# Output projections of a two-layer trunk: rows 0 to 3 from full-float products to split products, with two vector operations moved to ScalarE

## The chip, the cores and the metric
The kernel runs on one core of one Trainium2 chip, in one launch. The metric is the device time of one execution in microseconds (us); the number given for a kernel is the median of its runs. Engines: PE is TensorE (PEld its weight loads), DVE is VectorE, ACT is ScalarE, POOL is GpSimd, and SP issues the DMAs.

## The reference, cut to what matters
The input is x of 256 positions by 1024 channels, all in float32. There are two layers, each a mixer and a squared-ReLU MLP with 4096 hidden channels, each behind an RMSNorm and with a residual add.

```
def mixer_ab(h, w_in, conv_w, ln_g, ln_b, w_out):      # layer 0
    u_val, u_gate, q, k, v = split(h @ w_in)           # 512 columns each
    ya = silu(layernorm(causal_conv31(u_val * sigmoid(u_gate)), ln_g, ln_b))
    yb = attention(q, k, v)                            # 8 heads of 64, causal, ALiBi
    return concatenate([ya, yb], -1) @ w_out           # 1024 x 1024

def mixer_c(h, w_in, conv_w, conv_b, ...):             # layer 1
    gate, xr = split(h @ w_in)                         # 1024 columns each
    xr = causal_conv4(xr, conv_w) + conv_b
    r, i = sigmoid(xr @ w_r + b_r), sigmoid(xr @ w_i + b_i)   # block diagonal, 8 x 128
    a = exp(-8 * r * softplus(-lam))
    y = scan(a, sqrt(1 - a * a) * (i * xr)) * gelu(gate)
    return y @ w_out                                   # 1024 x 1024

x = x + mixer(rmsnorm(x));  x = x + (relu(rmsnorm(x) @ w_up) ** 2) @ w_down
```

## The kernel before, in words
Activations lie transposed: a tile holds 128 channels by 256 positions, so that 1024 channels are eight tiles, numbered 0 to 7 (a "row" of a projection is one such tile of its input, and the 128 rows of the weight that belong to it). Weights come from HBM in pieces of 1 MB, two units of 512 KB each. In both output projections rows 0 to 3 are, in layer 0, the convolution's four tiles `y[c]` and, in layer 1, the first four tiles `gi[c]` of the recurrence; rows 4 to 7 of layer 0 are the attention's output.

**Two forms of product.** `mm` (line 685) multiplies one unit's tile with one activation tile. If the weight is a plain float32 tile it is one float32 matmul. If it is a pair (`wh`, `wl`) and the activation a pair (high, low), it is three matmuls of the type fp32r: `wh` by high, `wh` by low, `wl` by high. A pair is made in `weights` (line 565): per half unit a copy `wh<-raw` (128x512, by `move`, which either ACT or DVE can take) and a subtraction `wl<-raw,wh` on DVE. An activation's pair is made in `split_act` (line 708) in the same way, on 128x256.

**Where weights lie.** There are five buffers `raw` (NRAW, a whole piece each) and eight pairs of buffers `wh`/`wl` (NSPL), both used in rotation. `piece` (line 516) gives a piece a place: "raw" stays in a `raw` buffer unsplit; "split" lands in a `raw` buffer and then takes one `wh`/`wl` pair for each of its two units; "pair" lands, unsplit, with its first unit in a `wh` buffer and its second in the `wl` buffer beside it, and needs no `raw`. Before the change rows 4 to 7 of layer 0's output projection are "split", and rows 0 to 3 of it and all eight rows of layer 1's are "pair".

**The order.** Nothing is issued as written. Each call records an operation with its reads, writes and a cost; a planner (`Plan`, line 50 on) then does list scheduling forward and backward for ten rounds, with a model of each engine's costs and of the DMA queue (one rate, DMA_RATE, for all transfers), and the best order by that model is emitted, each engine's queue strictly in that order. The weight DMAs keep the order in which they were written, on SP's queue. PE's order is in the plan, too.

**Around the change.** Layer 0: four tiles of the 31-tap convolution run on DVE beside the projections and the attention; `ln` (line 929) takes mean and variance over channels with matmuls against `ones`, in between the output projection's rows 4 to 7 (`out_rows`), and ends with four Silu on ACT; then `out_cols` (line 961) runs over pairs of output tiles with rows 0 to 3 inside, and calls `residual_chunk` for each finished tile, which starts the MLP's norm. Layer 1: `xr_tail` (line 1099) is the four-tap convolution, `gates`, `recur_a` (line 1119), `recur_b`, `recur_c` are the recurrence, `gate_out` (line 1145) multiplies with the Gelu of the gate and gives `mx[c]`; then `out_rows` for rows 0 to 3 one after another and `out_cols` for rows 4 to 7. The MLP's first six up units (`up0` to `up5`) and its first down units take the `wh`/`wl` pairs that come next in the rotation.

**SBUF.** The eight tiles `xg` (x times the norm's gain, 128x256) are used by layer 0's input projections only.

Of the kernel before, what the change touches and what calls it, by code (L numbers as in the profile page):

```python
# [6 lines left out]
F32 = mybir.dt.float32  # L7
# [4 lines left out]
P = 128  # L12
S = 256
# [315 lines left out]
def hybrid_trunk(ctx, tc, x, mix_norm, mlp_norm, w_up, w_down, ab_w_in, ab_conv_w, ab_ln_g, ab_ln_b,  # L329
# [8 lines left out]
    def tl(name, shape=(P, S), dt=F32):  # L338
        return sb.tile(list(shape), dt, name=name)
# [5 lines left out]
    def act(out, in_, func, scale=1.0, bias=None, accum=None):  # L345
        kw = {}
        ins = [in_]
        c = 0.05 if is_psum(in_) else 0.092
        c += fsize(in_) * 0.000833
        for n, v in (("scale", scale), ("bias", bias)):  # L350
            if isap(v):
                ins.append(v)
                c += 0.093
            if v is not None:
                kw[n] = v
        outs = [out]
        if accum is not None:
            kw["accum_out"] = accum
            outs.append(accum)
            c += 0.093  # L360
        return plan.add("A", [("activation", (out, in_, func), kw)], outs, ins, {"A": c}, func)
# [4 lines left out]
    def tt(out, a, b, op, engs="V"):  # L366
        n = fsize(out)
        cost = {}
        if "V" in engs:
            cost["V"] = vcost(n)  # L370
        if "G" in engs:
            cost["G"] = 0.135 + n * 0.0021
        return plan.add(engs, [("tensor_tensor", (out, a, b), {"op": op})], [out], [a, b], cost)
# [17 lines left out]
    def move(out, a, scale=None):  # L391

        n, ap, far = fsize(out), scale is not None, not is_psum(a)

        def go(e, sub):
            if e is nc.scalar:
                return e.activation(sub(out), sub(a), AF.Copy, **({"scale": scale} if ap else {}))  # L397
            return e.tensor_scalar(sub(out), sub(a), scale, None, op0=OP.mult) if ap else e.tensor_copy(sub(out), sub(a))  # L398

        return plan.add("VA", [(go, (), {})], [out], [a] + ([scale] if ap else []),  # L400
                        {"V": vcost(n, far, ap), "A": (0.092 if far else 0.05) + n * 0.000833 + 0.093 * ap}, AF.Copy)
# [12 lines left out]
    def memset(out, v, engs="G"):  # L414
        return plan.add(engs, [("memset", (out, v), {})], [out], [], {engs: 0.1 + fsize(out) * 0.0005})

    def mms(items, after=()):

        calls, outs, ins, c = [], [], [], 0.0
        for o, l, r, st, sp in items:  # L420
            calls.append(("matmul", (o,), {"lhsT": l, "rhs": r, "start": st, "stop": sp, "skip_group_check": True}))
            outs.append(o)
            ins += [l, r]
            c += max(fsize(r) / 2400.0, 0.0533) * (1 if l.dtype == F32R else 4) + (0.0135 if l.dtype == F32R else 0.005)
        return plan.add("T", calls, outs[:1], ins, {"T": c}, after=after)
# [12 lines left out]

        return plan.add("G", [("dma_start", (out, in_), {})], [out], [in_], {"G": 0.55}, lag=4.0)

    def dma(out, in_, size):
        return plan.add("S", [("dma_start", (out, in_), {})], [out], [in_], {"S": 0.0}, size=size)


    ident = tl("ident", (P, P))
    ones = tl("ones", (P, P))
    pcol = tl("pcol", (P, P))
    wcol = tl("wcol", (P, P))
    eps_t = tl("eps", (P, 1))
# [3 lines left out]

    whs = [tl(f"wh{i}", (P, KD * P)) for i in range(NSPL)]
    wls = [tl(f"wl{i}", (P, KD * P)) for i in range(NSPL)]
    shared = {t.tensor.name: f"{n}{i}" for n, ts_ in (("wh", whs), ("wl", wls)) for i, t in enumerate(ts_)}
    plan.shared = {n: 0 for n in shared}

    def renew(name, form):
        return sb.tile([P, KD * P], F32R if form % 2 else F32, name=f"{shared[name]}_{form}", tag=shared[name])  # L460

    def take(t, part):

# [23 lines left out]
    def rot(tag, n=None, shape=(P, S), dt=F32):  # L487
        if tag not in pools:
            pools[tag] = [[tl(f"{tag}{i}", shape, dt) for i in range(n)], 0]
        p = pools[tag]  # L490
        t = p[0][p[1] % len(p[0])]
        p[1] += 1
        return t
# [45 lines left out]
    def rows(ap, place):  # L539
        return piece("r", ap, place)  # L540
# [4 lines left out]
    def load(n, lo=0, hi=KD):  # L545

        taken[1] = n + 1
        kind, ap = pieces[n]
        for j, home in enumerate(homes[n]):
            if home.tensor.name in shared:  # L550
                take(home, 0)
            if kind == "ri":
                dma(home.rearrange("p (k c) -> p k c", k=KD), (c_w_r, c_w_i)[j][0].rearrange("h i j -> i h j"), P * 4096)
                continue
            if kind == "gv":
                dma(home.rearrange("p (k c) -> p k c", k=KD)[:, lo:hi], ap[j][:, lo:hi], P * 512 * (hi - lo))
                continue
            h = ap.shape[1] // 2
            a, b = (j * h, j * h + h) if kind == "r" else (max(lo, j * h), min(hi, j * h + h))
            if a < b:  # L560
                dst = home.rearrange("p (a b) -> p a b", a=h)
                dma(dst[:, a - j * h:b - j * h], ap[:, a:b], P * 4096 * (b - a) // h)

    @plan.part
    def weights(u):
# [41 lines left out]
    wo = ab_w_out[0].rearrange("(k p) c -> p k c", p=P)  # L607
    u_o = {}
    for k in (4, 6, 0, 2):
        u_o[k], u_o[k + 1] = rows(wo[:, k:k + 2], "split" if k > 3 else "pair")  # L610
    LAG, TAIL = 4, 4

    def mlp_units(layer):
# [16 lines left out]
        u_gt += cols(c_w_in[0], c, "split")  # L630
    wco = c_w_out[0].rearrange("(k p) c -> p k c", p=P)
    for k in range(0, 8, 2):
        u_co += rows(wco[:, k:k + 2], "pair")
    u_up[1], u_dn[1] = mlp_units(1)


# [10 lines left out]
    R = lambda ap: ap.rearrange("a (b p) -> (a b) p", p=P)  # L647
    make_identity(nc, ident)
    memset(ones, 1.0, "V")
    memset(eps_t, EPS, "V")  # L650
    act(tiny[:, 60:61], eps_t, AF.Sqrt)

# [27 lines left out]
    def par(name, c):  # L680
        i = col0[name] + c
        return pcol[:, i:i + 1]
# [21 lines left out]
    def narrow(b, w, xs):  # L704
        for k in range(0, KD, 4):
            mms([(b[:, :S], w[1][:, j, :], xs[j][0], False, j == KD - 1) for j in range(k, k + 4)])

    def split_act(src, scale, tag, bufs, engs="V"):
        t = rot(tag, bufs, (P, 2 * S), F32R)
        h, lo = t[:, :S], t[:, S:]  # L710
        if scale is None:
            move(h, src)
            tt(lo, src, h.bitcast(F32), OP.subtract, engs)
        else:
            move(h, src, scale)
            stt(lo, src, scale, h.bitcast(F32), OP.mult, OP.subtract)
        return h, lo, t

    def scaled(src, scale):
        t = rot("xg", KD)  # L720
        move(t, src, scale)
        return t

    def residual_chunk(k, acc, gname, g0, xs):
        tt(xT[k], acc, xT[k], OP.add)
# [20 lines left out]
    def x_chunk(k):  # L746
        b = bank("a")
        transposes([(b[:, t * P:(t + 1) * P], xrow[k * XP // KD][:, t, k % (KD // XP) * P:(k % (KD // XP) + 1) * P], ident) for t in range(2)])
        xs[k] = scaled(b[:, :S], par("mix", k))
        move(xT[k], b[:, :S])  # L750

    for k in range(KD):
# [175 lines left out]
    @plan.part  # L928
    def ln():
        tt(mean, y[0], y[1], OP.add)  # L930
        tt(mean, mean, y[2], OP.add)
        b = bank("b")
        mms([(b[:, :S], ones, mean, True, False)])
        mms([(b[:, :S], ones, y[3], False, True)])
        act(mean, b[:, :S], AF.Copy, scale=1.0 / 512)
        sq = [ssum, rot("nsq", 2), sumb, rot("nsq", 2)]
        for c in range(4):
            tt(y[c], y[c], mean, OP.subtract)
            act(sq[c], y[c], AF.Square)
            if c % 2:  # L940
                tt(sq[c - 1], sq[c - 1], sq[c], OP.add)
        b = bank("b")
        mms([(b[:, :S], ones, ssum, True, False)])
        mms([(b[:, :S], ones, sumb, False, True)])
        act(mean, b[:, :S], AF.Sqrt, scale=1.0 / 512, bias=eps_t)
        recip(mean, mean)
        for c in range(4):
            tt(y[c], y[c], mean, OP.mult)
            act(y[c], y[c], AF.Silu, scale=par("lng", c), bias=par("lnb", c))
            mx[c] = y[c]  # L950

    def accumulators():
        t = [bank("a") for _ in range(4)]
# [145 lines left out]
    def xr_tail(c, b):  # L1099
        xp = xps[c % 2]  # L1100
        tt(xp[:, 3:], b[:, :S], rstd, OP.mult)
        t = ar(S)
        ts(t, xp[:, 0:S], par("cw", c), par("cb", c), OP.mult, OP.add)
        for j in range(1, 4):
            stt(t, xp[:, j:j + S], par("cw", j * KD + c), t, OP.mult, OP.add)
        xc[c] = t
# [12 lines left out]
    def recur_a(c):  # L1119

        a = arot("ga", 8, S)
        act(a, gr[c], AF.Exp, scale=neg4[:, c:c + 1], bias=neg4[:, c:c + 1])
        act(gr[c], gr[c], AF.Tanh, scale=pos4[:, c:c + 1], bias=pos4[:, c:c + 1])
        a2 = arot("a2", 2, S)
        tt(a2, a, a, OP.mult)
        stt(gr[c], a2, 1.0, gr[c], OP.add, OP.mult)
        stt(gi[c], gi[c], 1.0, xc[c], OP.add, OP.mult)
        ga[c] = a
# [16 lines left out]
    def gate_out(c):  # L1145
        act(ym[c], ym[c], AF.Gelu_apprx_tanh)
        tt(gi[c], ym[c], xc[c], OP.mult)
        mx[c] = gi[c]

    b0, b1 = xr_proj(0), xr_proj(1)  # L1150
    finish_norm()
# [112 lines left out]
```

## Time and profile before

| | |
|---|---|
| median of 3 runs | 568.79 us (568.79 to 569.5) |
| the profiled execution | 569.07 us |
| its span, from first to last instruction | 567.3 us |
| mean granted TensorE clock | 0.998 |
| PE, PEld | 558.9 us (99%), 482.2 us (85%) |
| DVE, ACT | 415.4 us (73%), 310.9 us (55%) |
| HBM read | 97.11 MB |

The busy shares are over the whole span; single stages differ from them. The granted clock is 1.00 in every slice but the last, that is, the 2.4 GHz level. A float32 matmul stands in the trace as two matmul records. Since matmuls are pipelined and their ends are modelled, the durations of single matmuls overlap, and a pace is better read from a stretch of time and a count. Most lines have the number L312, that of the helper that issues recorded operations, so groups are told apart by tiles. ("Identity" and "Square" in the change are functions of ACT's activate instruction.)

### The profile page before, as it was taken

The page shows a single profiled execution, that of the slowest core. Times are in us where ns is not written, and L with a number is a line of the kernel's source. Part 1 is how long each engine was busy: PE and PEld are TensorE (multiplying, and loading weights), DVE is VectorE, ACT ScalarE, POOL GpSimd, SP SyncE. Part 2 cuts the span into 40 slices and gives each one's busy share as a digit, 9 for nine tenths or more (in the row PEclk, how much of TensorE's full clock was granted, in tenths as well). Part 3 has the DMA queues.
Part 4 walks back from the last instruction along what each step waited for, and adds up shares of the span by engine and source line. Part 5 has one row for each costly group of instructions (what it writes and reads, how often), then busy time and mean ns, then how long its engine had stood idle before and what let it go on. Part 6 is the DMA issues. An engine that isn't in the chain of part 4 may idle for free.

```text
span 567.3 us, 8519 instructions
## 1 busy us (share of the span) xinstructions
PE 558.9 (99%) x2985; PEld 482.2 (85%) x2985; DVE 415.4 (73%) x962; ACT 310.9 (55%) x641; POOL 7.5 (1%) x31
## 2 busy tenths in 40 slices
PE   8999999999999999999999999999999999999995
PEld 7887849988888888888889999888888888888884
DVE  2899998889766765776649999869677667757722
ACT  5104134667655656565537797728555655565623
POOL 5000000000000000000000000000000000000000
PEclk9999999999999999999999999999999999999999
DMA  8991493316666566565009738945656665662001
GB/s 241 283 375 73 138 323 134 122 56 193 196 209 192 172 200 197 175 197 174 0 1 278 242 123 280 370 157 156 199 167 191 210 192 172 202 203 93 1 1 75
DMA packets 71739, 98.71 MB, mean 174 GB/s; under 512 B 3368, under 2 KB 59776, under 8 KB 71696
## 3 DMA queue, kind: packets, MB, share of 16 engines
q1 hardware_dynamic: 71408, 98.06, 55.0%
q8 instruction: 23, 0.38, 0.3%
q14 instruction: 20, 0.16, 0.1%
q0 software_dynamic: 288, 0.11, 0.1%
HBM read 97.11 MB, written 1.05 MB: 173 GB/s over the span
## 4 chain that ended last, share of the span: by engine, by line
PE 94%; DMA 3%; DVE 2%; issue 1%; SPq 0%; ACT 0%; DVEq 0%; ACTq 0%
PE bank_b L312 50%; PE bank_a L312 44%; DMA raw<-in_ab_w_out_dram 2%; DVE arena L312 1%; DMA arena<-in_x_dram 1%; DVE wl L312 0%; SPq L312 0%; ACT arena L312 0%; ACT wh L397 0%; DVE xg L398 0%; DVE x L398 0%; DVE x L312 0%; DVE xT L398 0%; ACT tiny L312 0%; DVE tiny L312 0%
## 5 line engine op out<-in xcount | busy, mean ns | idle before, releaser
L312 DVE TENSOR_TENSOR wl<-raw,wh 128x512 fp32r<-128x512 f32 x296 | 197.0, 687 | 97.5 <-PE bank_b L312 75.6
L397 ACT ACTIVATE wh<-raw 128x512 fp32r<-128x512 f32 x265 | 163.8, 629 | 114.7 <-PE bank_a L312 53.7
L312 PE MATMUL bank_b<-x,wh 128*128 128x512 f32 (+1 forms) x768 | 169.7, 356 | 0.0
L312 PE MATMUL bank_a<-wh,f 128*128 128x512 f32 x512 | 158.5, 391 | 0.0
L312 PEld LDWEIGHTS bank_b<-x,wh 128*128 128x128 f32 x768 | 136.3, 189 | 20.3
L312 PEld LDWEIGHTS bank_a<-wh,f 128*128 128x128 f32 x512 | 94.2, 188 | 18.1
L312 PE MATMUL bank_b<-x,wl 128*128 128x256 f32 x640 | 102.6, 283 | 0.0
L312 PE MATMUL bank_a<-wl,f 128*128 128x512 f32 x256 | 99.6, 389 | 0.0
L312 PEld LDWEIGHTS bank_b<-x,wl 128*128 128x128 f32 x640 | 90.2, 191 | 2.5
L312 PEld LDWEIGHTS bank_a<-wl,f 128*128 128x128 f32 x256 | 48.1, 188 | 10.2
L312 DVE SCALAR_TENSOR_TENSOR arena<-arena,wcol 128x256 f32<-128x256 f32 x120 | 50.7, 484 | 0.2
L312 ACT ACTIVATE relu<-bank_b 128x256 f32<-128x256 f32 x64 | 24.5, 383 | 32.0 <-PE bank_b L312 30.4
L312 PE MATMUL bank_b<-xg,raw 128*128 128x256 f32 x160 | 35.8, 380 | 0.0
L312 PEld LDWEIGHTS bank_b<-xg,raw 128*128 128x128 f32 x160 | 29.9, 190 | 3.9
L312 ACT ACTIVATE relu<-relu 128x256 f32<-128x256 f32 x64 | 23.7, 410 | 17.1 <-DVE relu L312 17.0
L312 DVE TENSOR_TENSOR relu<-bank_b,relu 128x256 f32<-128x256 f32 x64 | 26.6, 419 | 3.9 <-ACT relu L312 3.9
L312 ACT ACTIVATE arena<-arena 128x256 f32<-128x256 f32 (+2 forms) x39 | 18.8, 522 | 16.2 <-DVE arena L312 15.6
L312 PE MATMUL bank_a<-arena,wl 128*128 128x256 f32 x96 | 26.3, 379 | 0.0
L312 PE MATMUL bank_a<-arena,wh 128*128 128x256 f32 x96 | 26.3, 379 | 0.0
L312 DVE TENSOR_TENSOR f<-relu,f 128x256 fp32r<-128x256 f32 x64 | 25.3, 419 | 0.5 <-ACT f L397 0.5
L312 DVE SCALAR_TENSOR_TENSOR relu<-relu,rstd 128x256 f32<-128x256 f32 x64 | 24.4, 419 | 0.1
L312 DVE TENSOR_TENSOR xT<-bank_a,xT 128x256 f32<-128x256 f32 x24 | 8.9, 419 | 15.8 <-PE bank_a L312 15.8
(127 smaller groups left out, 443.6 us busy)
## 6 DMA issues: line engine op xcount, KB each, us to landing
raw<-in_w_up_dram SPq DMA_DIRECT2D x64, 512.0 KB, 4.5
raw<-in_w_down_dram SPq DMA_DIRECT2D x64, 512.0 KB, 4.3
raw<-in_c_w_in_dram SPq DMA_DIRECT2D x16, 512.0 KB, 7.0
raw<-in_ab_w_in_dram SPq DMA_DIRECT2D x8, 512.0 KB, 8.1
wh<-in_ab_w_in_dram SPq DMA_DIRECT2D x5, 512.0 KB, 9.2
wl<-in_ab_w_in_dram SPq DMA_DIRECT2D x5, 512.0 KB, 9.6
raw<-in_ab_w_out_dram SPq DMA_DIRECT2D x4, 512.0 KB, 10.5
wh<-in_c_w_out_dram SPq DMA_DIRECT2D x4, 512.0 KB, 3.4
```

The source lines that it names most:

```text
L312: r.append(getattr(self.engines[o.eng], method)(*map(sub, a), **{n: sub(v) for n, v in k.items()}))
L397: return e.activation(sub(out), sub(a), AF.Copy, **({"scale": scale} if ap else {}))
```

## The change
Four things change. (1) Rows 0 to 3 of both output projections become "split", and their activations become pairs, so that each of their products is three fp32r matmuls instead of one float32 matmul. The activation pairs lie in four tiles `xg` of 128x512, which replace the eight of 128x256. (2) In `ln` the mean's division by 512 moves into the matmul's `ones_c` tile, and the subtraction reads the mean from PSUM. (3) The first tap of layer 1's convolution goes from a DVE tensor_scalar to an ACT activation, and so does the square of the decay. (4) In the planner's model a DMA's size is multiplied by a factor that depends on the length of its contiguous rows.

```diff
-    def dma(out, in_, size):
+    def dma(out, in_, size, line=4096):
+
+        size *= {512: 1.24, 1024: 1.02, 2048: 0.95}.get(line, 0.9)
...
-    ones = tl("ones", (P, P))
+    ones, ones_c = tl("ones", (P, P)), tl("ones_c", (P, P))
...
+    xgs = [tl(f"xg{i}", (P, 2 * S)) for i in range(4)]
+    shared = {t.tensor.name: (f"{n}{i}", list(t.shape)) for n, ts_ in (("wh", whs), ("wl", wls), ("xg", xgs))
+              for i, t in enumerate(ts_)}
...
-        u_o[k], u_o[k + 1] = rows(wo[:, k:k + 2], "split" if k > 3 else "pair")
+        u_o[k], u_o[k + 1] = rows(wo[:, k:k + 2], "split")
...
-    u_co += rows(wco[:, k:k + 2], "pair")
+    u_co += rows(wco[:, k:k + 2], "split" if k < 4 else "pair")
...
     memset(ones, 1.0, "V")
+    memset(ones_c, 1.0 / 512)
...
     def split_act(src, scale, tag, bufs, engs="V"):
-        t = rot(tag, bufs, (P, 2 * S), F32R)
+        if tag == "m":
+            t = xgs[next(turns)]
+            take(t, 1)
+            t = t.bitcast(F32R)
+        else:
+            t = rot(tag, bufs, (P, 2 * S), F32R)
...
-        mms([(b[:, :S], ones, mean, True, False)])
-        mms([(b[:, :S], ones, y[3], False, True)])
-        act(mean, b[:, :S], AF.Copy, scale=1.0 / 512)
+        mms([(b[:, :S], ones_c, mean, True, False)])
+        mms([(b[:, :S], ones_c, y[3], False, True)])
...
-            tt(y[c], y[c], mean, OP.subtract)
+            tt(y[c], y[c], b[:, :S], OP.subtract)
...
-            mx[c] = y[c]
+            mx[c] = split_act(y[c], None, "m", 4)
...
-        ts(t, xp[:, 0:S], par("cw", c), par("cb", c), OP.mult, OP.add)
+        act(t, xp[:, 0:S], AF.Identity, scale=par("cw", c), bias=par("cb", c))
...
-        tt(a2, a, a, OP.mult)
+        act(a2, a, AF.Square)
...
-        mx[c] = gi[c]
+        mx[c] = split_act(gi[c], None, "m", 4) if c < 4 else gi[c]
```

## Rows read from the trace of the kernel before

**Rows 1.** The page: busy time by engine (first line), shares of the chain of waits.

```profile
PE 558.9 (99%) x2985; PEld 482.2 (85%) x2985; DVE 415.4 (73%) x962; ACT 310.9 (55%) x641; POOL 7.5 (1%) x31
PE 94%; DMA 3%; DVE 2%; issue 1%; SPq 0%; ACT 0%; DVEq 0%; ACTq 0%
```

**Rows 2.** Windows: stretch, its length, busy PE PEld DVE ACT POOL, clock, DMA share, GB/s.

```profile
103.14:109.25 6.11, 6.11 (x53) 6.11 (x52) 6.02 (x12) 4.48 (x7) 0.00 (x0) 1.00 0.49 141
109.25:122.96 13.71, 13.71 (x66) 11.79 (x65) 9.64 (x26) 5.26 (x14) 0.00 (x0) 1.00 0.26 92
355.48:383.16 27.68, 27.68 (x130) 24.18 (x129) 21.14 (x49) 13.78 (x28) 0.00 (x0) 1.00 0.74 258
84.00:109.25 25.25, 25.16 (x192) 23.58 (x192) 22.58 (x81) 14.75 (x37) 0.00 (x0) 1.00 0.36 120
123.00:146.00 23.00, 23.00 (x126) 19.96 (x125) 22.52 (x48) 17.66 (x38) 0.00 (x0) 1.00 0.58 180
306.00:319.30 13.30, 13.30 (x105) 13.03 (x104) 13.03 (x30) 8.54 (x15) 0.00 (x0) 1.00 1.09 349
319.30:351.20 31.90, 31.69 (x245) 30.69 (x244) 30.76 (x74) 31.61 (x58) 0.00 (x0) 1.00 0.52 174
```

**Rows 3.** Groups by form: engine, tiles, shapes, count | busy us, mean ns | idle before.

```profile
L312 PE MATMUL bank_a<-arena,wh 128*128 128x256 f32 x96 | 26.3, 379 | 0.0
L312 DVE TENSOR_TENSOR wl<-raw,wh 128x512 fp32r<-128x512 f32 x296 | 197.0, 687 | 97.5 <-PE bank_b L312 75.6 <-ACT wh L397 18.0 <-PE bank_a L312 3.6
L397 ACT ACTIVATE wh<-raw 128x512 fp32r<-128x512 f32 x265 | 163.8, 629 | 114.7 <-PE bank_a L312 53.7 <-PE bank_b L312 36.9 <-DMA raw<-in_ab_w_out_dram 9.0
L397 ACT ACTIVATE f<-relu 128x256 fp32r<-128x256 f32 x53 | 19.3, 402 | 0.1
L398 DVE CAST f<-relu 128x256 fp32r<-128x256 f32 x11 | 3.2, 290 | 0.0
L312 DVE TENSOR_TENSOR arena<-arena 128x256 f32<-128x256 f32 x34 | 13.1, 418 | 1.6 <-ACT arena L312 1.5
L312 DVE TENSOR_SCALAR arena<-arena,pcol 128x256 f32<-128x256 f32 x8 | 3.1, 414 | 0.0
L312 ACT ACTIVATE arena<-arena,pcol 128x256 f32<-128x256 f32 x4 | 2.1, 591 | 0.0
L312 ACT ACTIVATE nsq<-xT 128x256 f32<-128x256 f32 x18 | 6.7, 401 | 0.0
L312 PEld LDWEIGHTS bank_a<-x,wh 128*128 128x128 f32 x64 | 10.0, 191 | 0.3
```

**Rows 4.** Timeline of PE, first products of layer 0's `out_cols`: start, length, operation, count.

```profile
109.25 0.60 PE L312 MATMUL bank_a<-arena,wh 128*128 128x256 f32 x2
```

**Rows 5.** Timeline of ACT and DVE in layer 0's layer norm.

```profile
98.58 0.38 ACT L312 ACTIVATE arena<-bank_b 128x256 f32<-128x256 f32 x1 [2.73 <-PE bank_b L312]
99.00 1.43 DVE L312 TENSOR_TENSOR arena<-arena 128x256 f32<-128x256 f32 x4 [0.39 <-ACT arena L312]
108.40 2.08 ACT L312 ACTIVATE arena<-arena,pcol 128x256 f32<-128x256 f32 x4
```

**Rows 6.** Waits: who waited for whom, us in total, times, longest.

```profile
PE bank_b L312 <- DVE arena L312: 0.7, 1, 0.7
ACT wh L397 <- DMA raw<-in_ab_w_out_dram: 9.0, 1, 9.0
```

**Rows 7.** Timeline of DVE: last `wl` before and first after layer 0's `out_cols`.

```profile
109.69 1.28 DVE L312 TENSOR_TENSOR wl<-raw,wh 128x512 fp32r<-128x512 f32 x2
122.75 0.69 DVE L312 TENSOR_TENSOR wl<-raw,wh 128x512 fp32r<-128x512 f32 x1
```

**Rows 8.** Timeline of ACT, DVE and PE where layer 1's output projection begins.

```profile
350.44 0.73 ACT L312 ACTIVATE arena<-arena 128x256 f32<-128x256 f32 x2
354.28 1.15 ACT L397 ACTIVATE wh<-raw 128x512 fp32r<-128x512 f32 x2 [3.10 <-DMA raw<-in_w_up_dram]
355.32 3.62 PE L312 MATMUL bank_a<-arena,wh 128*128 128x256 f32 x16
```

More of the change, by code (lines that the diff above doesn't have):

```diff
@@ L455, in hybrid_trunk @@
     wls = [tl(f"wl{i}", (P, KD * P)) for i in range(NSPL)]
-    shared = {t.tensor.name: f"{n}{i}" for n, ts_ in (("wh", whs), ("wl", wls)) for i, t in enumerate(ts_)}
+    xgs = [tl(f"xg{i}", (P, 2 * S)) for i in range(4)]
+    shared = {t.tensor.name: (f"{n}{i}", list(t.shape)) for n, ts_ in (("wh", whs), ("wl", wls), ("xg", xgs))
+              for i, t in enumerate(ts_)}
     plan.shared = {n: 0 for n in shared}
     def renew(name, form):
-        return sb.tile([P, KD * P], F32R if form % 2 else F32, name=f"{shared[name]}_{form}", tag=shared[name])
+        tag, shape = shared[name]
+        return sb.tile(shape, F32R if form % 2 else F32, name=f"{tag}_{form}", tag=tag)
     def take(t, part):
@@ L552, in load @@
             if kind == "ri":
-                dma(home.rearrange("p (k c) -> p k c", k=KD), (c_w_r, c_w_i)[j][0].rearrange("h i j -> i h j"), P * 4096)
+                dma(home.rearrange("p (k c) -> p k c", k=KD), (c_w_r, c_w_i)[j][0].rearrange("h i j -> i h j"), P * 4096, 512)
                 continue
             if kind == "gv":
-                dma(home.rearrange("p (k c) -> p k c", k=KD)[:, lo:hi], ap[j][:, lo:hi], P * 512 * (hi - lo))
+                dma(home.rearrange("p (k c) -> p k c", k=KD)[:, lo:hi], ap[j][:, lo:hi], P * 512 * (hi - lo), 512)
                 continue
@@ L561, in load @@
                 dst = home.rearrange("p (a b) -> p a b", a=h)
-                dma(dst[:, a - j * h:b - j * h], ap[:, a:b], P * 4096 * (b - a) // h)
+                dma(dst[:, a - j * h:b - j * h], ap[:, a:b], P * 4096 * (b - a) // h, ap.shape[2] * 4)
     @plan.part
@@ L706, in narrow @@
             mms([(b[:, :S], w[1][:, j, :], xs[j][0], False, j == KD - 1) for j in range(k, k + 4)])
+    turns = (i % len(xgs) for i in range(1000))
     def split_act(src, scale, tag, bufs, engs="V"):
-        t = rot(tag, bufs, (P, 2 * S), F32R)
+        if tag == "m":
[4 more added lines that the diff above has]
+            t = rot(tag, bufs, (P, 2 * S), F32R)
         h, lo = t[:, :S], t[:, S:]
@@ L717, in split_act @@
         return h, lo, t
[L719 to L722, printed above, removed]
     def residual_chunk(k, acc, gname, g0, xs):
@@ L748, in x_chunk @@
         transposes([(b[:, t * P:(t + 1) * P], xrow[k * XP // KD][:, t, k % (KD // XP) * P:(k % (KD // XP) + 1) * P], ident) for t in range(2)])
-        xs[k] = scaled(b[:, :S], par("mix", k))
+        xs[k] = xgs[k // 2][:, k % 2 * S:(k % 2 + 1) * S]
+        move(xs[k], b[:, :S], par("mix", k))
         move(xT[k], b[:, :S])
```

## Prediction
> **What bounds the kernel now.** I read the page first, then the chain of waits, then windows of single stages, then groups by form, then timelines of the three places that the change touches. The page has PE busy for 558.9 us of the 567.3 us span, and 94% of the chain that ended last lies on PE [rows 1]. So time is gained where PE's own work gets shorter, and lost where something else arrives late at PE. The windows show how near the others are. In layer 0's rows 4 to 7 and norm (84 to 109.25 us) DVE is busy for 22.58 us of 25.25; where the MLP begins (123 to 146) for 22.52 of 23.0; in layer 1's mixer DVE has 13.03 of 13.30 and ACT 8.54, and then, from 319.3 to 351.2, DVE 30.76 and ACT 31.61 of 31.90 [rows 2]. Yet PE is busy in all of these: both helpers arrive just in time, and there is little room for more work on them. That is the conflict of this change: it makes PE's work shorter and gives DVE and ACT more.
>
> **The products, part (1).** Layer 0's `out_cols` runs from 109.25 to 122.96 us, 13.71 us for four rows by eight output tiles, 32 float32 products of 0.428 us; layer 1's eight rows take 27.68 us for 64, 0.4325 us each [rows 2]. (The group counts agree: 96 records with `wh` and as many with `wl`, two records to a product, are 96 products [rows 3].) The price of the new form stands in the same matrix: rows 6 and 7 of layer 0, already split, run from 103.14 to 109.25 us, 17 groups of three matmuls in 6.11 us, 0.3594 us a group [rows 2, 4]. So 32 products cost 32 x 0.3594 = 11.50 us. Layer 0: 13.71 - 11.50 = 2.21 us less. Layer 1, half of 27.68: 13.84 - 11.50 = 2.34 us less. Together **-4.55 us**, all on PE and so on the path, as far as the operands are there.
>
> **What the split adds.** In each layer four units are split: 8 copies `wh<-raw` (0.63 us alone; two in a row take 1.15, so 0.52 when back to back [rows 3, 8]) and 8 subtractions `wl` (0.687; two take 1.28, so 0.60 [rows 3, 7]): 4.2 us, on ACT unless the plan gives some to DVE, and 4.8 us on DVE. Four activation pairs add four copies (0.29 on DVE or 0.40 on ACT) and four subtractions (0.42; four in a row take 1.43, so 0.34 [rows 3, 5]): 1.3 us on DVE. That is 6.1 us of DVE and some 5.5 of ACT per layer. The bytes moved stay the same.
>
> In layer 0 nothing pays for it except idle time. DVE has 25.25 - 22.58 = 2.7 us idle before `out_cols` and 13.71 - 9.64 = 4.1 us within it [rows 2], 6.8 us against 6.1. It fits only because six units of the MLP (`up0` to `up5`) are split before the first product of the MLP now [rows 7], which is earlier than it needs them: PE goes through two such units in 5.5 us. The rotation forces this anyway: by counting the pairs, `up4`, `up5` and the first two down units come to lie where rows 0 to 3 lay, and can be split only when `out_cols` is over. PE has `up0` to `up3` by then, 11 us of work, and the two late units want 4 x 0.60 = 2.4 us of DVE. I cost this at nothing; if the cover fails, it is rival A.
>
> **Layer 0's norm, part (2).** The ACT copy of the mean goes: from its start at 98.58 to the first subtraction at 99.00 are 0.42 us [rows 5]. Behind the four Silu come now the pairs. The last Silu would end at 108.40 + 2.08 - 0.42 = 110.06, its high part at 110.35 (a DVE cast of 0.29), its low part at 110.77. PE, free at 109.25 as now, asks for row 3's high part at 109.25 + 3 x 0.36 = 110.33 and for the low part 0.12 later. So the pairs are some 0.3 us late. Best case 0; worst, if the norm starts no earlier (0.42) and a `wl` of 0.69 stands in the queue ahead of two of the pairs, 0.3 + 0.42 + 1.4 = 2.1. I take **+0.4 us**, near the end that the rows give directly.
>
> **Layer 1's mixer, parts (1) and (3).** DVE gives away 8 first taps (0.414, some 0.33 back to back) and 8 squares (0.418, 0.34) [rows 3, 5]: 5.4 us against the 6.1 it gets. ACT takes 8 activations with two columns as operands; the Silu has that form, 0.591 us, and (2.08 - 0.59) / 3 = 0.50 back to back [rows 3, 5], so 4.0 us; 8 Squares of 0.40, some 0.31 back to back, 2.5 us; and 5.5 us for the pairs: 12 us. ACT's idle time there is 4.8 us before 319.3 and 3.1 us just before 354.28, where it waits for an MLP weight [rows 2, 8]; but a copy can go to DVE (0.29 for an activation [rows 3]), and the splits of the MLP's first units, at 354.28 and after, can wait: PE wants them at 383. The last rows' activations have 13 us between the first product at 355.3 and their own. So what decides is the pair of row 0, whose copy and subtraction (0.40 + 0.42) stand between `gate_out` and PE. I take half of that, **+0.4 us**; from below -0.2 (DVE is relieved, and PE's 31.69 busy us of 31.90 leave no more to win [rows 2]), from above rival B's 7.3.
>
> **The plan's rates, part (4).** These move no byte; they move instructions. At 33 to 43 us ACT stood 9.0 us in its queue for a DMA that the plan thought earlier, DVE stood behind it, and PE waited 0.7 us for DVE [rows 6]. A plan with slower short rows expects that DMA later, but how much of the wait this removes the trace cannot show: between -0.7 and, if another instruction stands in the wrong place instead, +0.7. I take **-0.2 us**. `ones_c` costs one memset on POOL, which is busy 1% [rows 1]: nothing.
>
> **The sum**, against the profiled execution's own 569.07 us (span 567.3 and 1.77 around it): -4.55 + 0.4 + 0.4 - 0.2 = -3.95, which is 565.1. The median of the runs lies 0.28 below the profiled one, so **564.8 us**.
>
> **Rivals.**
> *A: layer 0's DVE is too late.* If the plan puts the 8 `wl` and 4 low parts (6.1 us) ahead of the norm's end instead of the MLP's splits, with 2.7 us of idle time there, the pairs come 3.4 us late in place of 0.4: 564.8 + 3.0 = 567.8. For it: DVE at 89% before 109.25 and 98% after 123 [rows 2]. Against it: the six units that can wait [rows 7].
> *B: layer 1's ACT becomes the bound, and the change is slower.* Place: the stretch from 319.3 to the first product at 355.3. Five of the eight first taps fall there (5 x 0.50), the 8 Squares (2.5), the 8 copies of weights (4.2) and four of activations (4 x 0.31): 10.4 us into an engine that is 99% busy; the idle 3.1 us before 354.28 take some, 7.3 us stay, and PE has nothing else to do once the last projection chunk is through: 564.8 - 0.4 + 7.3 = 571.7. It decides against the change from the point where the Gelus are more than about 4.5 us later than now. For it: ACT's 31.61 of 31.90 us [rows 2]. Against it: copies can go to DVE, which loses 5.4 us, and only the first row is needed at 355. The Trainium skill, "ScalarE: Activation LUTs", section "Rules for kernel authors", would have multiplies and adds on VectorE and not on ScalarE, which is this rival's side; the trace agrees as to the single instruction (0.59 against 0.41 us [rows 3]), but shows DVE the fuller one before 319.3 [rows 2].
> *C: the three products don't come at 0.36 us.* Weight loads are 100% busy in the stretch I take the price from, and three loads replace two records' worth of them. If with the new tiles each product waited out a load of 0.191 us [rows 3], the 64 triples would cost 64 x (0.573 - 0.43) = 9.2 us more than now: 569.07 - 0.28 + 9.2 = 578.0. Against it: the same tiles in the same matrix run at the price taken, with loads 100% busy [rows 2]. The Trainium skill, "Trainium Kernel Development and Optimization", section "Best Practices", would have the weight loads' busy share judged rather than the matmuls'; by that the split rows are at their limit, but that limit is already in the 0.3594.
>
> **How the numbers follow.** Forecast 0.70 (its own range 563.7 to 566.8, from the terms' ends other than the rivals'); A 0.14, of which 0.04 ends faster still; B 0.13, of which 0.03 comes out even; C 0.03. A measurement of this kernel can tell about 0.2%, 1.1 us, from no change. Faster is then 0.70 + 0.04 = 0.74, the same 0.10 + 0.03 = 0.13, slower 0.10 + 0.03 = 0.13. For the range I leave 0.04 below (a new plan that happens to remove more waits than the rows show) and some 0.15 above, most of B and C: 563.6 to 568.6.
>
> **What would show it.** Right: both output projections' rows 0 to 3 at 11.5 us on PE, gapless; 16 more `wl` subtractions (312); PE's busy time near 554.4; its idle time within 1 us of now. Wrong: a gap of PE ahead of layer 0's `out_cols` waiting for DVE (A); a gap after the last gate chunk, waiting for ACT, with the Gelus late (B); triples at over 0.4 us (C). The forecast fails as well if the reordered plan opens gaps in the MLPs, where nothing was changed.

## The result, and the profile after

The changed kernel takes **565.55 us** (median of 4 runs, 565.41 to 565.69) against 569.1 us for the kernel before in the same comparison (4 runs, 568.79 to 569.5): a ratio of 0.9939 with a 95% interval of 0.9924 to 0.9955. Timed once more on another occasion it took 565.67 us against 568.83 (0.9939, 0.9926 to 0.9951). The forecast was 564.8 us, faster, in a range of 563.6 to 568.6. The profiled execution took 565.69 us, its span is 563.9 us; before it was 567.3.

The page after, busy time by engine and shares of the chain, which answers to [rows 1]:

```profile
PE 555.2 (98%) x3049; PEld 482.3 (86%) x3049; DVE 421.0 (75%) x973; ACT 323.0 (57%) x674; POOL 7.7 (1%) x32
PE 89%; DVE 4%; DMA 4%; SPq 1%; ACT 1%; issue 0%; ACTq 0%
```

PE is busy 3.7 us less, and the span is 3.4 us shorter: nearly all that PE saved arrived at the end. To see where, I cut the span at the first PE operation of each stage (the last cuts are the end of VectorE's last operation and the end of the span). Windows of the changed kernel by these cuts (stretch, length, busy PE PEld DVE ACT POOL, clock, DMA share, GB/s), from layer 0's first v product on:

```profile
69.35:109.20 39.85, 39.61 (x227) 29.95 (x227) 37.55 (x119) 22.18 (x55) 0.10 (x1) 1.00 0.35 116
109.20:120.72 11.52, 11.52 (x98) 11.52 (x97) 10.69 (x29) 6.62 (x16) 0.00 (x0) 1.00 0.32 104
120.72:298.18 177.46, 177.46 (x908) 152.01 (x907) 123.10 (x259) 106.51 (x216) 0.00 (x0) 1.00 0.50 161
298.18:353.33 55.15, 54.70 (x428) 53.42 (x426) 51.20 (x118) 49.15 (x102) 0.00 (x0) 1.00 0.67 217
353.33:378.52 25.19, 25.19 (x163) 23.46 (x161) 24.12 (x55) 15.12 (x34) 0.00 (x0) 1.00 0.97 337
378.52:559.28 180.76, 178.67 (x916) 152.89 (x914) 118.22 (x243) 103.35 (x212) 0.00 (x0) 1.00 0.45 143
559.28:563.90 4.62, 0.00 (x0) 0.00 (x0) 0.00 (x1) 0.00 (x0) 0.00 (x0) 0.58 0.32 115
```

The same cuts in every kernel of the study, lengths in us (all that follows is read against this table; the kernels e1 to e11 come below):

| kernel | start | v, attention | layer 0, rows 0-3 | MLP 0 | mixer 1 | projection 1 | MLP 1 | last store | span |
|---|---|---|---|---|---|---|---|---|---|
| before | 69.72 | 39.53 | 13.71 | 177.66 | 54.70 | 27.49 | 180.76 | 3.73 | 567.3 |
| changed | 69.35 | 39.85 | 11.52 | 177.46 | 55.15 | 25.19 | 180.76 | 4.62 | 563.9 |
| changed, again | 69.14 | 39.86 | 11.52 | 177.47 | 55.36 | 25.19 | 180.76 | 4.60 | 563.9 |
| e1 products only | 69.66 | 39.46 | 11.51 | 177.49 | 55.06 | 27.15 | 181.23 | 3.74 | 565.3 |
| e2 no rates | 69.87 | 39.95 | 11.52 | 177.46 | 56.00 | 25.19 | 180.77 | 3.74 | 564.5 |
| e3 nothing to ACT | 69.19 | 39.86 | 11.52 | 177.46 | 54.22 | 29.51 | 180.75 | 3.69 | 566.2 |
| e4 no products | 69.38 | 39.71 | 13.63 | 177.67 | 55.58 | 27.49 | 180.77 | 3.67 | 567.9 |
| e5 layer 1 only | 69.39 | 39.71 | 13.63 | 177.67 | 55.43 | 25.19 | 182.16 | 3.72 | 566.9 |
| e6 layer 0 only | 69.27 | 39.86 | 11.52 | 177.46 | 55.79 | 27.48 | 180.77 | 3.75 | 565.9 |
| e7 eight rows | 69.08 | 39.86 | 11.51 | 177.47 | 54.92 | 23.04 | 182.94 | 3.68 | 562.5 |
| e8 six rows | 69.20 | 39.86 | 11.52 | 177.46 | 54.22 | 23.97 | 183.24 | 3.73 | 563.2 |
| e9 stores first | 71.49 | 39.86 | 11.52 | 177.46 | 55.26 | 25.19 | 180.77 | 3.75 | 565.3 |
| e10 copies first | 70.86 | 39.86 | 11.51 | 177.47 | 54.98 | 25.18 | 180.77 | 4.67 | 565.3 |
| e11 stores in a gap | 69.03 | 39.87 | 11.52 | 177.46 | 55.14 | 25.18 | 180.77 | 3.73 | 562.7 |

From before to changed the stages give -0.37, +0.32, -2.19, -0.20, +0.45, -2.30, 0.00 and +0.89, together -3.40. The two shortened projections are -4.49 of it. The rest is +1.09, and most of that is at the very end, where nothing was changed.

Groups by form of the changed kernel, answering to [rows 3]:

```profile
L312 DVE TENSOR_TENSOR wl<-raw,wh 128x512 fp32r<-128x512 f32 x312 | 206.9, 688 | 92.2 <-PE bank_b L312 72.6 <-ACT wh L397 18.2 <-PE bank_a L312 1.3
L312 PE MATMUL bank_a<-xg,wh 128*128 128x256 f32 x128 | 23.1, 283 | 0.0
L312 ACT ACTIVATE arena<-arena,pcol 128x256 f32<-128x256 f32 x12 | 6.7, 595 | 1.0 <-DVE arena L312 1.0
```

The 312 subtractions are 16 more than before; the products now read `xg`, the activation pairs; and the twelve activations with a column are the four Silu of before and the eight first taps, at 0.595 us in the mean.

The timeline of VectorE and ScalarE in layer 0's norm (the subtraction of the mean, now from PSUM, and the Silu; then the last low parts and the next `wl`), which answers to [rows 5, 7]:

```profile
96.14 1.41 DVE L312 TENSOR_TENSOR arena<-arena,bank_b 128x256 f32<-128x256 f32 x4
105.71 2.08 ACT L312 ACTIVATE arena<-arena,pcol 128x256 f32<-128x256 f32 x4
...
108.71 0.76 DVE L312 TENSOR_TENSOR xg<-arena,xg 128x256 fp32r<-128x256 f32 x2
109.38 2.50 DVE L312 TENSOR_TENSOR wl<-raw,wh 128x512 fp32r<-128x512 f32 x4
```

And PE's first triple, which answers to [rows 4]:

```profile
109.20 0.40 PE L312 MATMUL bank_a<-xg,wh 128*128 128x256 f32 x2
109.44 0.28 PE L312 MATMUL bank_a<-xg,wl 128*128 128x256 f32 x1
109.56 0.40 PE L312 MATMUL bank_a<-xg,wh 128*128 128x256 f32 x2
```

A triple starts each 0.36 us, with no gap. The Silu begin 2.69 us earlier than before (105.71 against 108.40), and the last low part is there at 109.47, well before PE's fourth triple wants it.

Who PE waits for in the changed kernel (in total, times, longest), all waits that the view lists:

```profile
PE bank_a L312 <- DVE eps L312: 1.1, 1, 1.1
PE bank_b L312 <- DVE wl L312: 0.5, 1, 0.5
PE bank_a L312 <- DMA arena<-in_x_dram: 0.3, 1, 0.3
PE bank_b L312 <- DVE arena L312: 0.2, 1, 0.2
```

The first and the third lie at the start of the kernel, the fourth at 89.45 us in layer 0's attention. The second is in layer 1's mixer (at 339.08 us, in the timeline of PE):

```profile
339.08 0.38 PE L312 MATMUL bank_b<-x,wl 128*128 128x256 f32 x1 [0.45 <-DVE wl L312]
```

### The profile page after: what moved, and what is told of

It reads as the page before. It is cut to its first block, busy times and chain, and to the rows that moved or that the text cites. A ratio compares the mean times of both kernels' runs of the same rounds, so it can differ in the third digit from the quotient of the medians.

```text
span 563.9 us, 8676 instructions
## 1 busy us (share of the span) xinstructions
PE 555.2 (98%) x3049; PEld 482.3 (86%) x3049; DVE 421.0 (75%) x973; ACT 323.0 (57%) x674; POOL 7.7 (1%) x32
## 4 chain that ended last, share of the span: by engine, by line
PE 89%; DVE 4%; DMA 4%; SPq 1%; ACT 1%; issue 0%; ACTq 0%
PE bank_b L312 47%; PE bank_a L312 42%; DMA raw<-in_c_w_in_dram 3%; DVE arena L312 2%; DVE wl L312 2%; DMA arena<-in_x_dram 1%; SPq L312 1%; ACT L312 0%; ACT arena L312 0%; DVE wh L398 0%; ACT wh L397 0%; ACT tiny L312 0%; DVE tiny L312 0%; ACTq L312 0%; ACTq L397 0%
## 5 line engine op out<-in xcount | busy, mean ns | idle before, releaser
L312 DVE TENSOR_TENSOR wl<-raw,wh 128x512 fp32r<-128x512 f32 x312 | 206.9, 688 | 92.2 <-PE bank_b L312 72.6
L397 ACT ACTIVATE wh<-raw 128x512 fp32r<-128x512 f32 x283 | 173.8, 629 | 115.1 <-PE bank_a L312 56.9
L312 ACT ACTIVATE arena<-arena 128x256 f32<-128x256 f32 (+2 forms) x47 | 21.2, 500 | 17.3 <-DVE arena L312 16.9
L312 PE MATMUL bank_a<-xg,wh 128*128 128x256 f32 x128 | 23.1, 283 | 0.0
L312 PEld LDWEIGHTS bank_a<-xg,wh 128*128 128x128 f32 x128 | 20.0, 192 | 0.0
L397 ACT ACTIVATE f<-relu 128x256 fp32r<-128x256 f32 x53 | 19.4, 403 | 0.2
```

What stands on the lines that cost most here:

```text
L312: r.append(getattr(self.engines[o.eng], method)(*map(sub, a), **{n: sub(v) for n, v in k.items()}))
```

## The experiments

My theory after the result: the gain is PE's shorter products and nothing else; the edits to the norm, the mixer and the plan move tenths of a microsecond, those to ScalarE rather the wrong way. The rival: one of the small edits carries a part of the gain, because it gives VectorE the time for the splits.

**e1: the products alone.** Parts (2), (3) and (4) are undone (the edit against the changed kernel, cut).

```
-        size *= {512: 1.24, 1024: 1.02, 2048: 0.95}.get(line, 0.9)
-        act(t, xp[:, 0:S], AF.Identity, scale=par("cw", c), bias=par("cb", c))
+        ts(t, xp[:, 0:S], par("cw", c), par("cb", c), OP.mult, OP.add)
-        act(a2, a, AF.Square)
+        tt(a2, a, a, OP.mult)
...
```

> The kernel before with part (1) alone: rows 0 to 3 as three products; the norm's mean, the first tap, the square and the plan's rates stay as before. Theory (PE's shorter products carry the gain): the two output projections take 11.5 and 25.2 us as in the changed kernel, and the time is 565 to 566.5. Rival R1 (the plan's rates carry part of it): 567 or more, with the wait of some 0.7 us near 45 us still there. Rival R2 (ScalarE's two operations make the room on VectorE that the split needs): layer 1's mixer takes 57 us or more in place of 55.15, and the time is 567.5 or more.

Measured 567.37 us against 568.64 for before (0.9976, 0.9967 to 0.9985). That is only 1.3 us gained. Layer 0 has its 2.2 us, but layer 1's projection takes 27.15 us in place of 25.19. The timeline of PE in it shows why (in brackets the wait ahead of the matmul):

```profile
365.37 0.39 PE L312 MATMUL bank_a<-xg,wl 128*128 128x256 f32 x1 [1.71 <-DVE wl L312]
```

A low weight of rows 0 to 3 is late on VectorE, and PE stands in the middle of the projection. That is neither the time I expected (565 to 566.5) nor the rival's place: the mixer is 55.06 us, and the loss comes behind it.

**e2: the changed kernel without the plan's rates** (the line `size *= ...` is taken out).

> The changed kernel with the plan's one DMA rate as before. Theory: within 0.7 us of the changed kernel, 565.0 to 566.3, projections unchanged. Rival R1: the wait near 45 us is back and the time is 566.3 to 567.

Measured 566.26 us (0.9960, 0.9947 to 0.9972), 0.6 to 0.7 more than the changed kernel. In the table it is 0.5 more at the start and 0.85 more in the mixer, less 0.88 for the last store. So the rates are worth about 0.6 us as timed, not clear of noise, since its interval and the changed kernel's overlap; without the last store, which has a cause of its own (below), the two traces differ by 1.5 us. The sign that rival R1 named is there: PE's wait for VectorE near 45 us, 0.71 us before the change and gone in the changed kernel, is 0.75 us again in e2, at 45.88 us.

**e3: the changed kernel with the first tap and the square back on VectorE.**

```
-        act(t, xp[:, 0:S], AF.Identity, scale=par("cw", c), bias=par("cb", c))
+        ts(t, xp[:, 0:S], par("cw", c), par("cb", c), OP.mult, OP.add)
-        act(a2, a, AF.Square)
+        tt(a2, a, a, OP.mult)
```

> The changed kernel with the first tap and the square back on VectorE: 5.4 us more for VectorE in layer 1's mixer, 6.5 us less for ScalarE. Theory (VectorE is the fuller engine there): the mixer grows from 55.15 us by 0.5 to 2.5, time 566 to 568. Rival B of the prediction (ScalarE is what makes PE wait there): the mixer shrinks to 54.7, time 565.1.

Measured 568.04 us (0.9989, 0.9981 to 0.9998): 2.4 us slower than the changed kernel. The mixer itself is 0.93 us shorter (54.22), where I had expected it to grow. That is no price of the two edits: e8, which has them, comes to 54.22 as well. But the projection takes 29.51 us, 4.3 more than in the changed kernel and more than with float32 products. PE's line in it, then VectorE's queue just before:

```profile
363.86 0.39 PE L312 MATMUL bank_a<-xg,wl 128*128 128x256 f32 x1 [2.57 <-DVE wl L312]
```

```profile
361.53 0.68 DVE L312 TENSOR_TENSOR_SCAN arena<-arena 128x256 f32<-128x256 f32 x1
362.13 0.40 DVE L312 TENSOR_TENSOR arena<-bank_b,rstd 128x256 f32<-128x256 f32 x1
362.45 0.75 DVE L312 TENSOR_TENSOR arena<-arena 128x256 f32<-128x256 f32 x2
363.12 0.69 DVE L312 TENSOR_TENSOR wl<-raw,wh 128x512 fp32r<-128x512 f32 x1
```

VectorE works without a pause there. The recurrence's scans and gates for rows 4 to 7 stand in its queue among the splits of rows 0 to 3, and it is still at them when PE has nothing else left. But that is only the end of the chain. VectorE's last pause before it was a wait for ScalarE, and the chain lies on ScalarE from 323.7 us until that pause ends:

```profile
352.01 0.43 DVE L312 TENSOR_TENSOR arena<-arena 128x256 f32<-128x256 f32 x1 [2.18 <-ACT arena L312]
```

ScalarE has 16 operations less to do in e3, and yet it is busy for 329.0 us in place of 323.0. The plan books a table load (`ACT_TABLE_LOAD` in the trace) where an activation's function belongs to another set than the one before it, and e3's order has more of them (e3's line, then the changed kernel's):

```profile
L312 ACT ACT_TABLE_LOAD x20 | 25.7, 1283 | 1.1 <-PEq L1259 0.7
L312 ACT ACT_TABLE_LOAD x12 | 15.4, 1283 | 0.9 <-PEq L1259 0.7
```

The eight more take 10.3 us, all in layer 1. So e3 differs from the changed kernel in two ways, in VectorE's work and in the order that the plan gave ScalarE, and it does not show which of them makes the low weight late.

PE's wait is 2.57 us; what are the other 1.75? Windows of e3 around it (the clock is the third number from the end):

```profile
361.00:364.00 3.00, 0.43 (x4) 0.23 (x3) 3.00 (x8) 2.96 (x6) 0.00 (x0) 1.00 1.08 373
364.00:366.00 2.00, 2.00 (x13) 2.00 (x14) 2.00 (x5) 1.91 (x5) 0.00 (x0) 0.68 1.03 387
366.00:368.00 2.00, 2.00 (x11) 2.00 (x11) 2.00 (x5) 2.00 (x5) 0.00 (x0) 0.50 0.84 241
368.00:370.00 2.00, 2.00 (x11) 1.78 (x10) 2.00 (x5) 1.79 (x4) 0.00 (x0) 0.97 0.69 203
```

After PE had stood nearly idle for 2.6 us, the granted clock fell to 0.50, the 1.2 GHz level, and was 0.97 again in 368 to 370 us: the wait was paid once as a wait and again as slow matmuls. e1's wait of 1.71 us had no such sequel (1.00 in all slices around it). e3's runs lie from 567.05 to 569.72, the three lowest (567.05 to 567.30) at a mean clock of 0.999 and the others at 0.991 to 0.996, so the clock did not fall in each of them; against those three the changed kernel is 1.5 us faster. Not all of this adds up: at the full clock the traced execution (568.01 us) would have taken 566.3, and no run of e3 is below 567.05. Where the runs at the full clock lose the other 0.8 us, no trace shows.

In the changed kernel the windows of the mixer show the relief where it was full (compare [rows 2], 306 to 319.3 us: VectorE 13.03, ScalarE 8.54):

```profile
306.00:319.30 13.30, 13.30 (x103) 13.00 (x103) 11.14 (x25) 10.90 (x21) 0.00 (x0) 1.00 1.08 346
```

**e4: the changed kernel without the products** (both projections' rows 0 to 3 "pair" again).

```
-        u_o[k], u_o[k + 1] = rows(wo[:, k:k + 2], "split")
+        u_o[k], u_o[k + 1] = rows(wo[:, k:k + 2], "split" if k > 3 else "pair")
-        u_co += rows(wco[:, k:k + 2], "split" if k < 4 else "pair")
+        u_co += rows(wco[:, k:k + 2], "pair")
...
```

> The changed kernel with rows 0 to 3 of both projections as float32 products again, all else as changed. Theory: PE's projections take 13.7 and 27.5 us again, and the time is that of the kernel before within 0.7 us (568.4 to 569.8). Rival R1 or R2 (the other parts carry a share): 567.5 or less.

Measured 569.71 us (1.0023, 1.0014 to 1.0032): slower than before by 1.1 us. The three small parts lose 0.88 us in the mixer, where PE now waits for VectorE's `arena` 0.90 us in one piece, and gain 0.3 us in the other stages together. Just ahead of that wait VectorE itself stood 4.62 us, for ScalarE, which does seven table loads from 338 to 351.4 us:

```profile
351.85 0.76 DVE L312 TENSOR_TENSOR arena<-arena 128x256 f32<-128x256 f32 x2 [4.62 <-ACT arena L312]
```

So part (1) alone gains 1.3 us (e1), the other three alone lose 1.1 (e4), and all together gain 3.2; of parts (3) and (4) it is (3) without which more is lost (e3, against e2), and part (2) was not taken out by itself. Why they go together is not separated from the plan's order: the changed kernel has 12 table loads and e2, e7 and e8 have 13, against 15 before, 16 in e5, 17 in e4 and e6, 19 in e1 and 20 in e3, and each of these has five of them before layer 1.

**The changed kernel once more, and one layer at a time.** Open was the last store: 4.62 us from VectorE's last operation to the end, where before and e1 to e4 have 3.67 to 3.74.

> The changed kernel once more, for its end: in its first profile the last of the four output stores landed 3.2 us after its issue, in five others 2.3. If that is one execution's matter, the stretch from the last VectorE operation to the end of the span is 3.7 us in place of 4.6, and the time 564.7 to 565.2; if it belongs to the kernel, 4.6 us and 565.4 to 565.7.

It was 4.60 us again, so my expectation that this was one execution's matter was wrong: it belongs to this kernel.

**e5** has the products in layer 1 only, **e6** in layer 0 only (the edits of e4, each for one layer).

> The changed kernel with layer 0's rows 0 to 3 as float32 products again. Theory (each projection's gain is PE's own and they add up): layer 0's projection back from 11.5 to 13.7 us, all else unchanged, 2.2 us slower than the changed kernel: 567.0 to 568.0. Rival (layer 0's split costs VectorE more elsewhere than it gives PE): within 1 us of the changed kernel.

> The changed kernel with layer 1's rows 0 to 3 as float32 products again. Theory: mixer and projection of layer 1 together 83.1 us, as in the run without any split, against 80.3: 2.7 us slower than the changed kernel, 567.5 to 568.5. Rival (the mixer's wait of 0.45 us came from the split): 2.3 less 0.45, 1.9 us slower, 566.8 to 567.3.

Measured 568.22 us (0.9985, 0.9976 to 0.9994) and 567.88 us (0.9981, 0.9973 to 0.9990). Each has its own projection's gain in the table to the hundredth (25.19, 11.52), and each loses elsewhere, where its order came out otherwise: e5 1.40 us at the start of layer 1's MLP, e6 1.09 us in the mixer. The gains of the halves, 0.6 and 0.95 us as timed, don't add up to the whole's 3.2. e6 came out in the range I gave, e5 just above its own (567.0 to 568.0). With the first tap and the square on ScalarE and no splits in layer 1 (e4, e6) the mixer is some 0.9 to 1.1 us longer than before, and e6 shows the same chain as e4: PE waits 1.23 us for VectorE at 350.93 us, and VectorE has just waited 3.17 us for ScalarE, with seven table loads from 336 to 349.7.

**e7: all eight rows of layer 1 as three products.** If the price of a product holds, the four other rows are worth another 2.3 us.

```
-        u_co += rows(wco[:, k:k + 2], "split" if k < 4 else "pair")
+        u_co += rows(wco[:, k:k + 2], "split")
-        mx[c] = split_act(gi[c], None, "m", 4) if c < 4 else gi[c]
+        mx[c] = split_act(gi[c], None, "m" if c < 4 else "f", LAG + 3)
```

> The changed kernel with all eight rows of layer 1's projection as three products. PE's work shrinks by another 32 x 0.073 = 2.3 us, VectorE gets another 6.1 us before the last rows are due. Theory T1 (room is left, since the MLP's first splits at 362 to 369 us can wait): mixer and projection together 78.0 to 79.3 us in place of 80.3, time 563.3 to 564.6. Rival T2 (VectorE is full, and each further split comes back as a wait of PE for a wl): a wait of 2 us or more inside the projection, time 565 to 568.

**e8: six rows** (two tiles `xg` more, rows 0 to 5 split).

> Six of the eight rows of layer 1's output projection as three products, layer 0 and all else as in the changed kernel. Theory 1 (each row so moved saves 0.55 us of TensorE, as long as VectorE's spare keeps up; with all eight it gave 4.4 us in the projection and lost 2.2 us at the start of the MLP): the projection takes 24.1 us, the MLP's start waits under 1 us, and the kernel takes 563.7 to 564.9 us. Rival (what is lost at the MLP's start is VectorE's fixed backlog of splits for layer 1's MLP, whatever the count beyond four): 565.2 to 565.8, with a wait for VectorE of 1 us or more at the MLP's start.

Measured: e7 564.28 us (0.9915, 0.9902 to 0.9929), e8 564.84 us (0.9930, 0.9916 to 0.9943). The projection gets shorter as priced, 25.19 to 23.97 to 23.04 us. But the MLP behind it gets longer by 2.48 us with six rows and 2.18 with eight. Windows of e7 at that place, and PE's line:

```profile
366.00:372.00 6.00, 6.00 (x52) 6.00 (x51) 6.00 (x12) 2.66 (x6) 0.00 (x0) 1.00 1.07 376
372.00:378.00 6.00, 4.98 (x38) 4.45 (x36) 6.00 (x16) 5.31 (x14) 0.00 (x0) 1.00 1.05 374
378.00:384.00 6.00, 5.57 (x28) 4.29 (x29) 6.00 (x17) 5.37 (x12) 0.00 (x0) 1.00 0.51 161
```

```profile
378.25 2.74 PE L312 MATMUL bank_b<-x,wh 128*128 128x512 f32 x10 [1.28 <-DVE x L312]
```

VectorE is busy all 6.00 us of each of these stretches; what it has late is `x`, the MLP's input. So the projection's further gain is given back at once. It isn't the buffers: e7 keeps the pairs of rows 4 to 7 in the MLP's buffers `f`, e8 in tiles of its own, and both lose. For six rows I had expected less loss than for eight; there was more, as the rival said, and e8's time still lies in my range only because its mixer came out 0.93 us shorter (54.22). e7 is the fastest kernel of this study, yet 0.94 us of the 1.4 by which its span is shorter than the changed kernel's is the last store alone.

**The last store.** The DMA view of the changed kernel, 558 to 562.7 us in 40 slices (busy tenths, GB/s, then the queues: packets, MB, share):

```profile
DMA  0000000000000000009999999999962010000000
GB/s 0 0 0 0 0 0 0 0 0 0 0 0 0 0 0 0 0 35 349 349 418 331 366 419 331 401 436 366 366 227 35 0 17 0 35 17 35 0 0 0
...
q1 hardware_dynamic: 288, 0.52, 30.6%
q14 instruction: 1, 0.01, 0.4%
```

One packet of a list of instructions (queue q14) is fetched in the window of the store's packets, and a handful of the store's packets come in singly afterwards. Profiles with 3.7 us have no such packet there. The Trainium skill, "DMA: Bandwidth & Descriptors", section "Queues, rings and completion order", has each DMA engine take turns between its queues packet by packet; that fits, and no run here shows the turns themselves. If the packet is the cause, shifting the right engine's list by some places must move it away.

**e9** puts 24 stores of a zero by VectorE ahead of all else, **e10** 24 copies by ScalarE.

```
     make_identity(nc, ident)
+    for _ in range(24):
+        nc.vector.memset(tiny[:, 62:63], 0.0)          # e10: nc.scalar.copy(tiny[:, 63:64], ident[:, :1])
```

> The changed kernel with 24 stores of a zero by VectorE into an unused column ahead of all else, so that each later instruction of VectorE lies 24 places further on in its list; the work is the same. Theory 1 (the changed kernel's last store lands 0.9 us late because a packet of an instruction list is fetched among its packets, and the list is VectorE's): the stretch from VectorE's last operation to the end goes from 4.6 back to 3.7 us, and the kernel takes 564.5 to 565.1 us. Rival (the list is another engine's, or the packet isn't the cause): it stays at 4.6 us, and the kernel takes 565.4 to 566.0.

> The changed kernel with 24 copies of a column by ScalarE into an unused column ahead of all else, so that each later instruction of ScalarE lies 24 places further on in its list; the work is the same. Theory 1 (the packet among the last store's is of ScalarE's list): the stretch from VectorE's last operation to the end goes from 4.6 back to 3.7 us, and the kernel takes 564.5 to 565.1 us. Rival (another engine's list, or the packet isn't the cause): it stays at 4.6 us, and the kernel takes 565.4 to 566.5, with the copies' own time at the start in it.

The last stretch of e9 is 3.75 us and no packet of instructions comes there; e10 keeps 4.67 us and its packet. So the packet goes with VectorE's list. Both totals missed, 566.97 us and 568.6 us: the added operations cost 2.14 and 1.51 us at the start, which I had not reckoned. e10's runs fall into two groups, 567.06 to 567.30 us (mean clock 0.996 to 0.999) and 568.60 to 569.08 (0.993 to 0.996); the trace is of the first. That the second lost its clock behind the new waits at the start, as e3 did, is a guess that no trace tests.

**e11** has the 24 stores behind VectorE's second operation, in a gap in which it waits 3.65 us for PE.

```
             done.append((o, r))
+            nv += o.eng == "V"
+            if o.eng == "V" and nv == 2:
+                for _ in range(24):
+                    self.engines["V"].memset(spare, 0.0)
```

> The changed kernel with VectorE's 24 stores of a zero put behind its first two operations, where it stands idle for 3.65 us (0.95 to 4.66 us; ahead of all else they cost 2.14 us of the start). Theory 1 (the late last store is a packet of VectorE's own list, and nothing else came with the shift): the last stretch is 3.7 instead of 4.6 us, every other stretch is that of the changed kernel within 0.3 us, the span is 562.8 to 563.4 us, and the kernel takes 564.5 to 565.0 us. Rival (the gain at the end is given back at the start, since the stores delay what follows them there): 565.3 us or more.

Measured 564.91 us (564.48 to 565.23; 0.9931, 0.9917 to 0.9945), against 565.37 to 565.89 for the changed kernel's own five runs. All stages are the changed kernel's within 0.02 us except the first (-0.32; -0.11 against the changed kernel's second trace) and the last (-0.89); I expected a span of 562.8 to 563.4 and got 562.7. The DMA view of the same window:

```profile
DMA  0000000000000005999999999992000000000000
GB/s 0 0 0 0 0 0 0 0 0 0 0 0 0 0 0 209 436 331 383 401 366 401 366 349 453 349 349 70 0 0 0 0 0 0 0 0 0 0 0 0
...
q1 hardware_dynamic: 288, 0.52, 29.9%
```

No packet of instructions, no stragglers. The pages agree: the three traces with the late store have 973 instructions on VectorE (the changed kernel twice, and e10), and none of the other eleven has (949 to 997, the nearest 971 in e2).

## Why the prediction was right, point by point

- **The products, -2.21 and -2.34.** Measured -2.19 and -2.30, gapless, at the 0.36 us that rows 6 and 7 had shown. The forecast rests on this step, and it held to 0.04 us because the price was taken from the same tiles in the same matrix. One reading in it was off: the stretch for layer 1 (355.48 to 383.16) runs to the recorded end of the last product, and from its first product to the MLP's first it is 27.49 us, which makes the term -2.24. Rival C is out.
- **Layer 0's norm, +0.4.** It did not come as argued. I let the Silu end 0.42 us earlier than before; the plan began the norm's subtraction 2.86 us earlier (96.14 against 99.00), and the pairs were in time. The stage as a whole did get 0.32 us longer, with one wait of 0.2 us for VectorE, while the start got 0.37 shorter. The cover that I named for the splits (the MLP's six units can wait) held: up to the MLP's first product VectorE does 26 `wl` against 21 before, though eight were added, so three of the MLP's have moved behind it, and the MLP loses nothing. Rival A is out.
- **The mixer, +0.4.** Measured +0.45 (+0.66 in the second trace), but by another way: not row 0's pair, which is in time, but a low weight that VectorE has 0.45 us late at 339 us. The size was luck.
- **What was under-valued: part (3) in layer 1.** I credited the 5.4 us taken off VectorE with at most 0.2, since PE had no idle time to win back. That is a look at the kernel as it was. With 6.1 us of splits added, the kernels without part (3) have PE stop for a low weight within the projection, for 2.57 us in e3 and 1.71 in e1; with it the changed kernel has no such wait. As timed that is 1.5 to 2.4 us. VectorE's load is one side of it: in e1 it works 21.6 us on end before that wait is over. ScalarE's table loads are the other, 20 and 19 in place of 12, and no run parts the two. My sum came out because it took the gain for granted and the condition happened to be met.
- **Rival B, ScalarE as the bound,** was priced at 7.3 us. In the changed kernel it did not come: at its projection's start PE waits for nothing. The number I left out is the table loads, which my 12 us for ScalarE took as they were; the plan made them three fewer than before, 3.8 us of ScalarE. Where it made them more, B's chain is there at a smaller price: PE waits 0.90 us in e4 and 1.23 in e6 for a VectorE that has waited for ScalarE. The Trainium skill, "ScalarE: Activation LUTs", section "Rules for kernel authors", would keep multiplies and adds on VectorE. By the single instruction the trace agrees (0.595 against 0.414 us); by the kernel e3 does not, though with its eight more table loads it is no clean test of the rule.
- **The rates, -0.2.** They are worth about -0.6 as timed (e2), with overlapping intervals. The wait for VectorE that I tied to them at 45 us is gone in the changed kernel and back in e2 (0.75 us), so this reading held. ScalarE's wait for its DMA, which I gave as the reason, does not follow: it is 9.0 us before, 7.0 in the changed kernel and 7.3 in e2.
- **Not foreseen: +0.89 us in the last store** (e9, e11). Without it the measured sum would have been -4.29 instead of -3.40, and with my -3.95 I should have been 0.3 us too careful instead of 0.6 too hopeful.
- **What would show it.** The projections at 11.5 us (11.52; 25.19 for layer 1's eight rows, of which four are now triples), 312 `wl`, idle time within 1 us (8.7 against 8.4): right. PE's busy time is 555.2, not 554.4: 0.6 us of it are at the start, where the changed kernel's stage is shorter all the same, so this number, of modelled ends, is no measure of tenths.

## What to carry to other kernels

Price a new form of work from a stretch of the same kernel that already runs it, with the same tiles; here that term held to 0.1 us. Then ask of every helper engine not how busy it is now but whether it still meets each due time with the new work on it; an edit that relieves it can be a condition of the gain, as here, where neither half was worth much alone. Where a planner sets the order, compare what it added as well, such as table loads, before a difference is put down to the edit. And cut two traces at the same landmarks before explaining anything: two thirds of what e7's span "won" over the changed kernel's lay in a stretch that no edit had touched.

## What the runs showed that I had not expected

- A packet of VectorE's instruction list that is fetched while the last output store is under way makes that store land 3.2 us after its issue in place of 2.3, and the kernel 0.9 us longer. It goes with the number of instructions that VectorE has before it: 24 more, in a gap, take it away (e11), and 24 more on ScalarE do not (e10). Differences of under 1 us between two versions can be this alone.
- A wait of 2.57 us of PE in the midst of full work cost 4.3 us in the traced execution, since the clock went to the 1.2 GHz level after it (0.50 in 366 to 368 us of e3), though PE was busy again; one of 1.71 us (e1) had no such sequel.
- Putting 16 operations back from ScalarE to VectorE made ScalarE busier, 329.0 us in place of 323.0, since the new order has eight table loads more, at 1.283 us each (e3).
